# The last expert place's rows by one-hot products, other rows summed while it runs, and a second mixer that begins block of tokens by block

## The chip, the cores and the metric

One core of a Trainium2 chip runs the whole program as one launch. The metric is device time in microseconds (us), lower is better. All arithmetic is fp32 in effect: most matrix products are made as three products of fp32r halves (a high part `h` and a low part `l` of each operand: h·h, h·l, l·h), which is why every weight page is first split by a ScalarE cast (`wh`) and a VectorE subtraction (`wl`).

## The reference, cut to what matters

Two blocks follow each other on 512 tokens of 1024 features. The part around the change is the end of the first block (32 experts, 4 per token) and the beginning of the second block's mixer:

```python
# first block: mixture of experts on h2 = rms_norm(x) * (1 + scale2) + shift2
gates = softmax(top_k(h2 @ w_router + b_router, 4))
for each expert e, for its tokens:
    gu = xe @ w_gate_up[e] + b_gate_up[e]
    g, u = minimum(gu[:, :D_FF], 7.0), clip(gu[:, D_FF:], -7.0, 7.0)
    y = ((u + 1.0) * (g * sigmoid(1.702 * g))) @ w_down[e] + b_down[e]
x = x + gate2 * (sum over a token's 4 experts of gate * y)

# second block: mixer
h = rms_norm_2(x, mix_norm_g)
u, q, k, v, f_logit, g_ssm, g_att = split(h @ w_in)
y_ssm = s5_branch(u, ...)                       # a scan over the tokens
y_att = forgetting_attention(norm(q), norm(k), v, f_logit, ...)
x = x + (sigmoid(g_ssm) * y_ssm + sigmoid(g_att) * y_att) @ w_out
x = x + peer_ffn(rms_norm_2(x), ...)
```

## The kernel before

The program has four phases, one after the other. Tokens lie in four blocks of 128 (`NB` = 4, `tb` 0 to 3), features in eight chunks of 128 (`KC`). Buffers of 4 KB per partition ("pages", 128x1024) come from one pool of 30, and a load or a result waits until a page is free.

**Phase 1** (first mixer) is put in order by a planner: `race` takes a number of generators (lanes) and emits next from the one whose engines are free first by its own clock. A further lane or another page held changes the order of all of them.

**Phase 2** (experts) streams 32 experts' weights from memory in a fixed order of 24 ticks per expert: each tick uses one page of weights (the gate/up and down products `gu`, `dn`), and `at(tick, function)` hangs further work on a tick. An expert's tokens are gathered by an indirect DMA from `h2d` into a tile `xg` (there are four, `xgs`), and its scaled rows `y` are scattered by an indirect DMA on GpSimd's queue to `ybuf` in DRAM, four places per token (`Expert.finish`, line 1304; its DMA at L1317). Behind the last expert stands a run-time loop for tokens beyond an expert's 128 places (`Overflow.rest`, L1515, the loop at L1519). It runs zero times here, but all engines and DMAs meet at its end: this is the barrier between the phases, and it needs the last scatter landed.

**Phase 3** (second mixer) begins behind that barrier. SyncE's queue issues 16 loads of 512 KB of `yk` (the rows in `ybuf`, four for each block of tokens; `expert_rows`, L1573) and then weight pages `wr` (L213). ScalarE's queue issues four small loads, `grow`, `qkg`, `fb`, `causal`. `combine` adds each block's four rows to `x` (`x2[tb]`), partly on GpSimd and partly on VectorE, and ScalarE squares the sum. `roots` makes the reciprocal root of the norm by 13 operations on 128x1 (tiles `nsq`, `nr0v`, `nr0a`, `nrs`), `norm` makes `xn`, `turn` transposes it on TensorE (`xnT`) and casts the high parts `hTh`, `lows` makes the low parts `hTl`. The string `START` is the order in which these are written: a = combine, r = roots, n = norm, t = turn, l = lows, w = the first weight split. Then come four chunks of `u` and one of the forget logits (all named `ft`, 24 products of 512 columns each), and then `weave`, which interleaves lanes by the rates in `W3`: the scan (`ssm_scan`: products `x` and `y`, `zr`, `zi`, `tmp`), two attention lanes (`qt`, `s`, `pt`, `ob`), and `pair(qr)` for four quarters of the heads. `pair(qr)` waits until quarter `qr` - 2 has been attended, makes q, k and v of its two heads (`qkv(i, qr)` with i = 0, 1, 2: 96 products of 256 columns each), and then the two gate chunks (`ft`). For i = 0 and 1 `qkv` ends with a norm on VectorE (`qssq`, `rqv`, `rqa`, `qrs`, `raw`). Behind the weave follow `z` and `wo`.

**Phase 4** is the PEER layer, which the change doesn't touch.

GpSimd prepares the scan's rotations (`pw`, `co`, `si`, 12 operations on 128x512) as soon as its own adds are done.

Of the kernel before, what the change touches and what calls it, by code (L numbers as in the profile page):

```python
# [18 lines left out]
P = 128  # L19
# [286 lines left out]
def phase1(K):  # L306
# [693 lines left out]
    nc.scalar.dma_start(out=br, in_=row_bcast(I["b_router"], NE))  # L1000
    B, A = [pair_b(h) for h in range(4)], [pair_a(p) for p in range(4)]
    race(K.clock, third(0), third(1), third(2), third(3), prefetch(), roots(0), roots(1), *[second(tb) for tb in range(NB)], ws.lane(WSA), split_out(), norms(), *(lane(B[0],A[0]),lane(B[1],A[1]),lane(B[2],A[2]),lane(B[3],A[3])), lane(chunks(), projects()), lane(mod_rows((0, 1, 2)), mod_rows((3,))), mods2())
# [16 lines left out]
START = "a0 r01 n0 t0 a1 l0 r12 n1 t1 a2 l1 r23 n2 t2 a3 l2 w0 r34 n3 t3 l3"  # L1019
# [4 lines left out]
SMALL = 0.07  # L1024
EXTRA = (5, 7)
# [190 lines left out]
class Expert:  # L1216


    def __init__(self, K, xg, rank, mv, rows, sel):
        self.K, self.xg, self.rank, self.mv, self.rows = K, xg, rank, mv, rows  # L1220
        self.sel = sel
# [7 lines left out]
    def lists(self):  # L1229
# [13 lines left out]
        nc.vector.tensor_scalar(self.tok, self.dst, 2, None, op0=ALU.logical_shift_right)  # L1243
        nc.gpsimd.indirect_dma_start(out=self.xg, out_offset=None, in_=K.h2d[:, :],  # L1244
# [59 lines left out]
    def finish(self, last=False):  # L1304
        K, nc = self.K, self.K.nc
        y = K.page(name="y")
# [8 lines left out]
        if FIN == 2 and not last:  # L1315
            nc.gpsimd.tensor_tensor(out=y, in0=y, in1=K.gate2, op=ALU.mult)
        st = nc.gpsimd.indirect_dma_start(out=self.rows, out_offset=bass.IndirectOffsetOnAxis(ap=self.dst[:, :1], axis=0),  # L1317
                                          in_=y, in_offset=None, bounds_check=4 * T - 1, oob_is_err=False)
        for o in (K.scat or []):
            K.tc.declare_no_dep(st.ins, o.ins, reason="rows of other (token, choice) pairs")  # L1320
        if K.scat is not None:
            K.scat.append(st)
# [52 lines left out]
def phase2(K, nexp=NE):  # L1375
# [10 lines left out]
    K.ybuf = K.drp.tile([4 * T, D], F32, name="ybuf")  # L1386
# [7 lines left out]
    def mk(e):  # L1394
        rank, mv, sel = (K.rank, K.mv, K.selE) if e < FIXED else (K.rank_p, K.mv_p, K.sel_p)
        sel = sel[:, e:e + 1].to_broadcast([P, P])
        ex[e] = [Expert(K, xgs[e % 3], lambda tb: rank[:, tb, e:e + 1], lambda tb: mv[:, tb, e, :], K.ybuf[:, :], sel)]
# [32 lines left out]

    for i in range(16):
        at(1 + i, step, order)
    at(16, mk, 2)
    for e in range(nexp + 1):
# [13 lines left out]
        for x in ex.get(e, []):  # L1448
# [4 lines left out]
            at(n0 + 24 + 17, x.finish, e == nexp - 1)  # L1453
        if e == 5:
# [28 lines left out]
    for _ in chain(params, db):  # L1483
        pass
    K.rank = K.mv = K.G = K.cnt = K.iota32 = K.idc = None
    K.sel_p = K.rank_p = K.mv_p = K.rank_2 = K.served = K.perm = None
    over.rest(xgs[0])


class Overflow:  # L1490
# [5 lines left out]
    def block(self, b, xg):  # L1496
# [16 lines left out]
        return Expert(K, xg, lambda tb: r4[:, tb, 0:1], lambda tb: mv[:, tb, :], K.ybuf[:, :], sel.to_broadcast([P, P]))  # L1513

    def rest(self, xg):  # L1515
        K, nc, tc = self.K, self.K.nc, self.K.tc
        K.scat = None
        nx = nc.values_load(K.nx[0:1, 0:1], min_val=0, max_val=NXB - 1, skip_runtime_bounds_check_because="a count of blocks")
        with tc.For_i(0, nx, 1) as b:  # L1519
# [18 lines left out]
            x.finish()  # L1538

# [26 lines left out]
def expert_rows(K):  # L1566

    out = []
    for tb in range(NB):
        ys = [K.page(name="yk") for _ in range(4)]  # L1570
        src = K.ybuf[tb * 512:(tb + 1) * 512, :].rearrange("(p k) d -> p k d", k=4)
        for k in range(4):
            K.nc.sync.dma_start(out=ys[k], in_=src[:, k, :])  # L1573
        out.append(ys)
    return out


def combine(K, tb, ys, ssq):

    nc, x = K.nc, K.x2[tb]  # L1580
    nc.gpsimd.tensor_tensor(out=x, in0=x, in1=ys[0], op=ALU.add)
    nc.gpsimd.tensor_tensor(out=ys[1], in0=ys[1], in1=ys[2], op=ALU.add)
    nc.vector.tensor_tensor(out=x, in0=x, in1=ys[1], op=ALU.add)
    for i in range(2):
        s = slice(i * 512, (i + 1) * 512)
        nc.vector.tensor_tensor(out=x[:, s], in0=x[:, s], in1=ys[3][:, s], op=ALU.add)
# [269 lines left out]
def phase3(K):  # L1856
# [126 lines left out]
    for c in range(4):  # L1983
        K.split(feat_chunk(), *uT[c])
# [660 lines left out]
```

## Time and profile before

| what | us |
|---|---|
| median of 3 runs | 3761.43 |
| lowest and highest of them | 3748.43, 3765.33 |
| the profiled execution's own time | 3763.79 |
| its span (first to last instruction) | 3762.0 |
| TensorE, VectorE busy in the span | 3390.4, 3237.6 |
| last product of the last expert to first product of the second mixer | 1780.8 to 1850.5 |
| second mixer's weave | 1879.6 to about 2270 |

The profile is of one execution. A row of the timeline gives a start, a duration, engine, line, operation and tiles (out<-in), the number of like instructions in a row, and in brackets how long the engine had idled before and what released it. A row of the windows gives the busy time of TensorE (PE), its weight loads (PEld), VectorE (DVE), ScalarE (ACT) and GpSimd (POOL), each with its number of instructions, then the granted TensorE clock (1.00 is 2.4 GHz, 0.50 is 1.2 GHz), the DMA engines' share and GB/s. Products overlap, so the distance between two starts, not the duration of one, is their cost in a row. Nearly all operations are issued by one helper and so carry line 84: they are told apart by tile names. SPq, ACTq and POOLq are the engines' DMA queues.

### The profile page before, as it was taken

Reading aid. Unit: us, or ns where it says so; the run is one execution under the profiler, and the core shown is the slowest. Engines: PE = TensorE matmul, PEld = TensorE weight load, DVE = VectorE, ACT = ScalarE, POOL = GpSimd, SP = SyncE. Lnnn points to the kernel's source line nnn. Section 1 sums busy time; section 2 is a strip of 40 time slices with the busy share of each in tenths; the row PEclk is TensorE's granted clock in tenths of the full one; section 3 lists DMA queues with packets and bytes.
Section 4 is the critical chain, followed back from the end, with each engine's and each line's share of the span. In section 5 each row is a group of like instructions: output and inputs, shape, how many; then the busy total and the mean of one; then the engine's idle time right before and its main releaser. Section 6 shows DMA issues by size and latency. Waiting matters only on the chain. (4 is left out here: it accounts for less than half of the span.)

```text
span 3762.0 us, 51865 instructions
## 1 busy us (share of the span) xinstructions
PE 3390.4 (90%) x17053; PEld 2884.7 (77%) x17053; DVE 3237.6 (86%) x5729; ACT 1845.3 (49%) x2684; POOL 1096.1 (29%) x742
## 2 busy tenths in 40 slices
PE   6788789898999999999488899899889889999999
PEld 6776667667777888887377777798889889888887
DVE  7888789999898999998688776499999986799988
ACT  3233367666665677776234453333344445333333
POOL 5545501101110111111334440023223230456554
PEclk8878889999999999999699899899999999999999
DMA  6224369888997899997511112366779787999997
GB/s 216 85 85 157 129 232 327 295 306 304 334 317 252 319 356 368 351 366 282 182 51 51 51 52 100 104 208 216 237 241 309 251 291 248 334 340 342 345 340 260
DMA packets 453989, 906.05 MB, mean 241 GB/s; under 512 B 37810, under 2 KB 188978, under 8 KB 453586
## 3 DMA queue, kind: packets, MB, share of 16 engines
q1 hardware_dynamic: 333488, 692.66, 53.0%
q0 software_dynamic: 46368, 151.03, 11.1%
q10 hardware_dynamic: 73858, 59.00, 4.7%
q8 instruction: 136, 2.23, 0.2%
q14 instruction: 139, 1.14, 0.1%
HBM read 845.42 MB, written 74.96 MB: 245 GB/s over the span
## 5 line engine op out<-in xcount | busy, mean ns | idle before, releaser
L84 DVE TENSOR_TENSOR wl<-wr,wh 128x1024 fp32r<-128x1024 f32 x1106 | 1346.4, 1252 | 150.9 <-ACT wh L84 145.1
L84 ACT CAST wh<-wr 128x1024 fp32r<-128x1024 f32 x1133 | 1132.8, 1049 | 166.7 <-DVE wl L84 44.0
L84 PE MATMUL ft<-HT,wh 128*128 128x384 f32 (+1 forms) x2304 | 620.7, 350 | 4.9 <-ACT wh L84 4.9
L84 PE MATMUL out<-wh,HT 128*128 128x512 f32 x1536 | 473.3, 389 | 1.5 <-ACT HT L84 1.5
L84 PE MATMUL gu<-wl,exh 128*128 128x512 f32 x1056 | 417.6, 395 | 22.5 <-DVE wl L84 22.3
L84 PEld LDWEIGHTS ft<-HT,wh 128*128 128x128 f32 x2304 | 424.4, 193 | 14.8 <-ACT wh L84 5.5
L84 PE MATMUL ft<-HT,wl 128*128 128x384 f32 (+1 forms) x1152 | 402.8, 350 | 26.0 <-DVE wl L84 25.8
L84 PE MATMUL gu<-wh,exh 128*128 128x512 f32 x1056 | 420.6, 398 | 0.3 <-ACT wh L84 0.3
L84 PE MATMUL gu<-wh,exl 128*128 128x512 f32 x1056 | 413.7, 392 | 0.0
L84 PEld LDWEIGHTS out<-wh,HT 128*128 128x128 f32 x1536 | 288.2, 188 | 61.9 <-ACT HT L84 1.8
L2454 POOL DMA_INDIRECT ug<-in_peer_u,et x128 | 167.6, 1309 | 453.5 <-DVE sv L84 241.5
L84 PE MATMUL out<-wl,HT 128*128 128x512 f32 x768 | 298.8, 389 | 0.0
L2454 POOL DMA_INDIRECT ug<-in_peer_v,et x128 | 156.3, 1221 | 362.0 <-DVE x L84 240.0
L84 PEld LDWEIGHTS gu<-wl,exh 128*128 128x128 f32 x1056 | 199.5, 189 | 74.8 <-DVE wl L84 35.6
L84 PEld LDWEIGHTS ft<-HT,wl 128*128 128x128 f32 x1152 | 221.8, 193 | 40.7 <-DVE wl L84 35.6
L1317 POOL DMA_INDIRECT ybuf<-y,dst x33 | 93.3, 2827 | 505.1 <-DVE y L84 505.1
L84 PE MATMUL qkv<-wl,hTh 128*128 128x256 f32 (+1 forms) x736 | 227.2, 309 | 14.4 <-DVE wl L84 11.8
L1244 POOL DMA_INDIRECT xg<-h2d,tok x33 | 42.9, 1300 | 675.8 <-PE dn L84 478.1
L84 PE MATMUL qkv<-wh,hTh 128*128 128x256 f32 (+1 forms) x736 | 235.1, 319 | 2.0 <-ACT wh L84 2.0
L84 PEld LDWEIGHTS gu<-wh,exh 128*128 128x128 f32 x1056 | 199.8, 189 | 45.7 <-ACT wh L84 3.0
L84 PE MATMUL dn<-wl,ath 128*128 128x512 f32 x528 | 213.5, 404 | 22.9 <-DVE wl L84 20.2
L84 PEld LDWEIGHTS gu<-wh,exl 128*128 128x128 f32 x1056 | 199.3, 189 | 41.8
(481 smaller groups left out, 6952.8 us busy)
## 6 DMA issues: line engine op xcount, KB each, us to landing
wr<-in_w_gate_up SPq DMA_DIRECT2D x512, 512.0 KB, 6.5
wr<-in_w_down SPq DMA_DIRECT2D x256, 512.0 KB, 6.4
wr<-in_u_t SPq DMA_DIRECT2D x128, 512.0 KB, 4.3
wr<-in_peer_v SPq DMA_DIRECT2D x128, 512.0 KB, 6.1
wr<-in_w_in SPq DMA_DIRECT2D x68, 512.0 KB, 3.5
wada<-in_w_ada SPq DMA_DIRECT2D x48, 512.0 KB, 4.3
Sd<-us ACTq DMA_DIRECT2D x128, 192.0 KB, 4.7
Gd<-gst ACTq DMA_DIRECT2D x12, 2048.0 KB, 15.7
```

Of the source, the lines that this page charges most:

```text
L84: return f(*a, **kw)
L1244: nc.gpsimd.indirect_dma_start(out=self.xg, out_offset=None, in_=K.h2d[:, :], in_offset=bass.IndirectOffsetOnAxis(ap=self.tok[:, :1], axis=0),
L1317: st = nc.gpsimd.indirect_dma_start(out=self.rows, out_offset=bass.IndirectOffsetOnAxis(ap=self.dst[:, :1], axis=0), in_=y, in_offset=None ...
L2454: nc.gpsimd.indirect_dma_start(out=r, out_offset=None, in_=tab, in_offset=bass.IndirectOffsetOnAxis(ap=et[:, m:m + 1], axis=0), bounds_che ...
```

## The change

1. **Zeros.** A lane of phase 1 fills one page with zeros and writes it 16 times (512 KB each, on SyncE's queue, paced 15 planner units apart) over `ybuf`, which is now made in phase 1. A place of `ybuf` that nobody scatters to therefore reads as zero.
2. **The last expert.** Its one-hot matrix is transposed by four TensorE transposes and a ScalarE copy into `xgs[3]`, its scaled rows go to `xgs[2]`, and its scatter is gone. Its part of each block's sum comes from fp32 products of the one-hot with the rows (`spread`, tiles `lt`, two products of 512 columns for each block).
3. **Loads ahead of the barrier.** In the last expert's ticks SyncE loads the rows of blocks 0 and 1 (`wind_up`), and VectorE adds them (`add_rows`): block 0's four ahead of the last `y`, block 1's four behind it and ahead of the barrier.
4. **Behind the barrier** the stream of phase 3 is made earlier (`stream3`): two weight pages, block 2's rows, two weight pages, block 3's rows, then the rest.
5. **`START`** is rewritten, with p = products, a = add the products and square, b = add the loaded rows, q = the q and k products of quarter 0 for one block of tokens, v = the first four `wl`. All adds are VectorE's.
6. **Order of the mixer.** Quarter 0's q, k and v stand ahead of the `u` chunks and the forget chunk and out of the weave; `pair(0)` makes its gates alone. The rates `W3` are unchanged.

VectorE from the last expert's down product to the first transposed block. `dn` is the down product, `yk` the loaded rows, `x` the sum of a block. Before:

```order
L84 SCALAR_TENSOR_TENSOR y_17256<-dn_17180,gate_16898,gate_3055 128x512
L1519 REGISTER_ALU
L1519 COMPARE_AND_BRANCH
L1519 UNCONDITIONAL_BRANCH
L84 SCALAR_TENSOR_TENSOR gq_17308<-qkg_17304 128x1
L84 TENSOR_TENSOR x_3047<-x_3047,yk_17273 128x1024
L84 TENSOR_TENSOR x_3047<-x_3047,yk_17275 128x512 x2
L84 TENSOR_TENSOR nsq_17333<-nssq_17324 128x1
```

The same place after, ahead of the barrier (the second fence stands behind it, at `gq`):

```order
L84 TENSOR_TENSOR x_3168<-x_3168,yk_16781 128x1024
L84 SCALAR_TENSOR_TENSOR xg_4130<-dn_16823,gate_15842,gate_3183 128x512
L84 SCALAR_TENSOR_TENSOR xg_4130<-dn_16824,gate_15842,gate_3183 128x512
L84 TENSOR_TENSOR x_3170<-x_3170,yk_16786 128x1024
L84 TENSOR_TENSOR x_3170<-x_3170,yk_16787 128x1024
L84 TENSOR_TENSOR x_3170<-x_3170,yk_16788 128x1024
L84 TENSOR_TENSOR x_3170<-x_3170,yk_16789 128x1024
L1568 TENSOR_LOAD nx_5761
```

```order
L84 SCALAR_TENSOR_TENSOR gq_17372<-qkg_17368 128x1
L84 TENSOR_TENSOR x_3168<-lt_17406,x_3168 128x512
L84 TENSOR_TENSOR x_3168<-lt_17407,x_3168 128x512
L84 TENSOR_TENSOR x_3170<-lt_17410,x_3170 128x512
L84 TENSOR_TENSOR x_3170<-lt_17411,x_3170 128x512
L84 TENSOR_TENSOR nsq_17432<-nssq_17384 128x2
```

VectorE's eight adds of blocks 0 and 1 have moved ahead of the barrier, and block 0's roots now stand behind the adds of eight products.

TensorE behind the barrier, before (`xnT` the transposes, `ft` the first `u` chunk):

```order
L1519 UNCONDITIONAL_BRANCH
L84 MATMUL xnT_17352<-ident_68,xn_17349 128x128 x4
L84 MATMUL xnT_17359<-ident_68,xn_17349 128x128 x4
...
L84 MATMUL xnT_17497<-ident_68,xn_17487 128x128 x4
L84 MATMUL ft_17521<-hTh_17312,wh_17465 128x512
```

and after (`xg` here are the last expert's rows and the one-hot, `qkv` the q and k products of the first block of tokens):

```order
L84 MATMUL lt_17406<-xg_4130,xg_4131 128x512
...
L84 MATMUL lt_17419<-xg_4130,xg_4131 128x512
L84 MATMUL xnT_17451<-ident_68,xn_17448 128x128 x4
L84 MATMUL xnT_17458<-ident_68,xn_17448 128x128 x4
L84 MATMUL xnT_17472<-ident_68,xn_17469 128x128 x4
L84 MATMUL xnT_17479<-ident_68,xn_17469 128x128 x4
L84 MATMUL qkv_17503<-wh_17386,hTh_17376 128x256
```

Eight products come ahead of the first transposes, and products of 256 columns begin when two blocks of tokens are transposed, not four.

TensorE in the first quarter's attention inside the weave, before (`pt` transposes the weights, `ob` multiplies them by v):

```order
L84 MATMUL pt_18733<-ident_68,e_18517 128x128
L84 MATMUL qkv_18616<-wh_18618,hTh_17316 128x256
L84 MATMUL qkv_18616<-wl_18619,hTh_17316 128x256
...
L84 MATMUL qkv_18617<-wh_18618,hTl_17319 128x256
L84 MATMUL ob_18725<-pt_18731,vh_18205 128x512
```

and after:

```order
L84 MATMUL pt_19015<-ident_68,spare_18125 128x128 x2
L84 MATMUL ob_18960<-pt_19007,vh_17934 128x384
...
L84 MATMUL pt_19051<-ident_68,spare_18125 128x128 x2
L84 MATMUL y_19058<-tmp_19009,cz_9111 32x512
L84 MATMUL y_19058<-tmp_19024,cz_9295 32x512
L84 MATMUL x_19064<-u_17941,bt_8329 128x512 x2
```

The 36 `qkv` products that stood between the transposes and the products with v are gone from there; between the last gate chunk and the end of this attention only the scan's `x` and `y` products stand beside it.

The diff, cut to its core:

```diff
+    def zeros():
+        z = K.page(name="zero")
+        v.memset(z, 0.0)
+        for i in range(16):
+            yield ZPACE * (i + 1)
+            nc.sync.dma_start(out=K.ybuf[i * P:(i + 1) * P, :], in_=z)
...
-START = "a0 r01 n0 t0 a1 l0 r12 n1 t1 a2 l1 r23 n2 t2 a3 l2 w0 r34 n3 t3 l3"
+START = "w0 p0 p1 p2 p3 a0 a1 r02 n0 t0 v0 n1 t1 l0 b2 a2 l1 q0 b3 a3 r24 n2 t2 q1 n3 t3 l2 l3 q2 q3"
...
+            for tb in range(NB):
+                nc.tensor.transpose(b[:, tb * P:(tb + 1) * P], self.ohs[:, tb, :].bitcast(F32), K.ident)
+            nc.scalar.copy(self.late[1], b)
...
+        if self.late is not None:
+            return
         st = nc.gpsimd.indirect_dma_start(out=self.rows, ...)
...
+    def spread(self, tb):
+        y, ohT = self.late
+        bs = [self.K.bank("lt") for _ in range(2)]
+        for i, b in enumerate(bs):
+            self.K.nc.tensor.matmul(b, ohT[:, tb * P:(tb + 1) * P], y[:, i * 512:(i + 1) * 512], start=True, stop=True)
+        return bs
...
+    def wind_up():
...
+        for tb in range(2):
+            rows[tb] = expert_rows(K, tb)
+    def add_rows(tb):
+        for y in rows.pop(tb):
+            nc.vector.tensor_tensor(out=K.x1[tb], in0=K.x1[tb], in1=y, op=ALU.add)
...
+        if e == nexp - 1:
+            at(n0 + 22, wind_up)
+            at(n0 + 24 + 8 + 6, add_rows, 0)
...
+    K.late = ex[nexp - 1][0]
+    add_rows(1)
     over.rest(xgs[0])
+    stream3(K)
+    for tb in range(2, NB):
+        for _ in range(2):
+            K.ws3.load()
+        rows[tb] = expert_rows(K, tb)
...
-def combine(K, tb, ys, ssq):
-    nc.gpsimd.tensor_tensor(out=x, in0=x, in1=ys[0], op=ALU.add)
-    nc.gpsimd.tensor_tensor(out=ys[1], in0=ys[1], in1=ys[2], op=ALU.add)
...
+    def total(tb):
+        x, sq = K.x2[tb], K.page(name="sq")
+        for i, b in enumerate(last.pop(tb)):
+            s = slice(i * 512, (i + 1) * 512)
+            nc.vector.tensor_tensor(out=x[:, s], in0=b, in1=x[:, s], op=ALU.add)
+            nc.scalar.activation(sq[:, s], x[:, s], AF.Square, accum_out=ssq[:, tb, i:i + 1])
...
+    for i in range(3):
+        for _ in qkv(i, 0):
+            pass
     up = [K.page(F32R, [P, 2, T], name="u") for _ in range(4)]
...
-        for i in range(3):
+        for i in range(3 if qr else 0):
             yield from qkv(i, qr)
```

## Rows read from the trace of the kernel before

**Rows 1.** Windows by stage; columns as told above.
```profile
0.00:500.00 500.00, 379.95 (x2154) 329.17 (x2154) 397.15 (x786) 176.28 (x374) 258.76 (x148) 0.82 0.39 134
1780.00:1850.00 70.00, 8.04 (x33) 5.98 (x32) 50.23 (x88) 10.17 (x29) 37.91 (x23) 0.54 0.52 187
```
**Rows 2.** Timeline of the seam between the phases.
```profile
1780.13 1.43 DVE L84 SCALAR_TENSOR_TENSOR y<-dn,gate,gate 128x512 f32<-128x512 f32 x2 [4.56 <-PE dn L84]
1781.83 0.98 POOL L1317 DMA_INDIRECT ybuf<-y,dst  x1 [15.72 <-DVE y L84]
1785.87 0.34 ACTq L1861 DMA_DIRECT2D grow<-in_mix_g_row  x1
1850.52 0.78 PE L84 MATMUL ft<-hTh,wh 128*128 128x512 f32 x1
```
**Rows 3.** Timeline: the tail of the last expert.
```profile
1758.73 7.39 POOL L1317 DMA_INDIRECT ybuf<-y,dst  x1 [32.66 <-DVE y L84]
1769.80 5.77 DVE L84 TENSOR_TENSOR wl<-wr,wh 128x1024 fp32r<-128x1024 f32 x5 [0.25 <-ACT wh L84]
```
**Rows 4.** DMA, 1757 to 1770 (GB/s in 40 slices), then issues with us to landing.
```profile
GB/s 416 378 416 340 366 340 315 353 403 416 403 416 403 403 403 403 378 202 63 38 0 0 0 0 25 0 0 0 0 101 429 378 202 101 0 0 0 50 0 0
ybuf<-y,dst POOLq DMA_INDIRECT x1, 9.6
yk<-ybuf SPq DMA_DIRECT2D x16, 512.0 KB, 9.0
grow<-in_mix_g_row ACTq DMA_DIRECT2D x1, 512.0 KB, 5.4
qkg<-in_qk_g ACTq DMA_DIRECT2D x1, 1.0 KB, 7.3
```
**Rows 5.** Timeline: adds (one of 1024, two of 512 columns) and a cast, GpSimd idle.
```profile
1832.51 2.55 DVE L84 TENSOR_TENSOR x<-x,yk 128x1024 f32<-128x1024 f32 x3
1843.39 1.03 ACT L84 CAST wh<-wr 128x1024 fp32r<-128x1024 f32 x1
```
**Rows 6.** Tile gm: fp32 products in phase 1 (min/median/max ns; first and last start).
```profile
L84 PE MATMUL gm<-gate,onesF x4: 592/592/644, 409.9 to 411.2; 128*128 128x512 f32 x4
```
**Rows 7.** Window: the clock some 3.5 us after dense products begin at 1850.5.
```profile
1854.00:1856.00 2.00, 2.00 (x10) 1.66 (x9) 1.17 (x1) 0.80 (x1) 0.00 (x0) 1.00 1.04 387
```
**Rows 8.** Timeline: roots and low parts beside GpSimd's operations, and alone.
```profile
1805.18 1.43 DVE L84 TENSOR_TENSOR nsq<-nssq 128x1 f32<-128x1 f32 x1 [0.79 <-ACT yk L84]
1815.48 3.18 DVE L84 SCALAR_TENSOR_TENSOR xn<-x,nrs,grow 128x512 f32<-128x512 f32 x2
1823.20 1.51 POOL L84 TENSOR_TENSOR tmp<-pw,pw 128x512 f32<-128x512 f32 x1
1823.71 1.40 DVE L84 TENSOR_TENSOR hTl<-xnT,hTh 128x256 fp32r<-128x256 f32 x4
1845.59 0.15 DVE L84 TENSOR_TENSOR nsq<-nssq 128x1 f32<-128x1 f32 x1
1848.09 1.41 DVE L84 SCALAR_TENSOR_TENSOR xn<-x,nrs,grow 128x512 f32<-128x512 f32 x2
```
**Rows 9.** Timeline: the first products of quarter 0, 24 in a row.
```profile
1879.59 0.28 PE L84 MATMUL qkv<-wh,hTh 128*128 128x256 f32 x1
...
1882.34 0.28 PE L84 MATMUL qkv<-wh,hTl 128*128 128x256 f32 x1
```
**Rows 10.** The weave: a VectorE group, first and last row of one norm, two windows.
```profile
L84 DVE TENSOR_TENSOR wl<-wr,wh 128x1024 fp32r<-128x1024 f32 x35 | 48.8, 1393 | 10.2 <-ACT wh L84 10.2
1899.68 1.27 DVE L84 TENSOR_REDUCE qssq<-tmp 128x4 f32<-128x512 f32 x2
1909.52 1.23 DVE L84 TENSOR_TENSOR raw<-raw,qrs 128x1024 f32<-128x1024 f32 x1
1880.00:1940.00 60.00, 48.22 (x296) 41.76 (x296) 53.47 (x73) 16.12 (x22) 19.46 (x16) 0.89 0.15 45
1940.00:2270.00 330.00, 306.36 (x1747) 249.34 (x1747) 253.40 (x450) 150.87 (x260) 140.33 (x98) 0.95 0.18 52
```

More of the change, by code (lines that the diff above doesn't have):

```diff
@@ L1305, in finish @@
         K, nc = self.K, self.K.nc
-        y = K.page(name="y")
+        y = self.late[0] if self.late is not None else K.page(name="y")
         for i in range(2):
@@ L1538, in rest @@
             x.finish()
+            for tb in range(NB):
+                for i, b in enumerate(x.spread(tb)):
+                    s = slice(i * 512, (i + 1) * 512)
+                    nc.vector.tensor_tensor(out=K.x1[tb][:, s], in0=b, in1=K.x1[tb][:, s], op=ALU.add)
 def down_bias(K):
@@ L1853, in norm_T, with stream3 @@
     return xn
-def phase3(K):
-    nc, I, tc = K.nc, K.I, K.tc
-    K.open_phase(K.ctx3, 3)
-    K.x2 = K.x1
-    grow = K.page(name="grow")
-    nc.scalar.dma_start(out=grow, in_=row_bcast(I["mix_g_row"], D))
-    rows = expert_rows(K)
-    qkg = K.small([P, 2], tag="qkg", bufs=1)
-    nc.scalar.dma_start(out=qkg, in_=I["qk_g_2"])
-    fb = K.const([40, 1], name="fb")
-    nc.scalar.dma_start(out=fb, in_=I["fbias"])
-    gq = K.const([P, 1], name="gq")
-    nc.vector.scalar_tensor_tensor(gq, qkg[:, 0:1], P ** -0.5, qkg[:, 1:2], op0=ALU.mult, op1=ALU.mult)
-    causal = K.const([P, T], name="causal")
-    nc.scalar.dma_start(out=causal, in_=I["causal"])
-    hT = [(K.page(F32R, [P, 2, T], "hTh"), K.page(F32R, [P, 2, T], "hTl")) for _ in range(4)]
-    def hTk(k):
-        return hT[k // 2][0][:, k % 2, :], hT[k // 2][1][:, k % 2, :]
+def stream3(K):
+    I = K.I
     w2 = I["w_in_2"]
@@ L1898, in phase3 @@
     UC, QC, KC0, VC, GS, GA = 0, 512, 1536, 2560, 3592, 4616
[L1899 removed]
+    srcs = []
     for qr in range(4):
@@ L1906, in phase3, with hTk @@
     srcs += [I["w_out_2"][k * P:(k + 1) * P, :] for k in range(KC)]
-    ws = WStream(K, srcs, 2, 1, late=True)
-    ws.load()
-    ws.load()
+    K.ws3 = WStream(K, srcs, 4, 4, late=True)
+def phase3(K):
+    nc, I, tc = K.nc, K.I, K.tc
+    K.open_phase(K.ctx3, 3)
+    K.x2 = K.x1
+    grow = K.page(name="grow")
+    nc.scalar.dma_start(out=grow, in_=row_bcast(I["mix_g_row"], D))
+    qkg = K.small([P, 2], tag="qkg", bufs=1)
+    nc.scalar.dma_start(out=qkg, in_=I["qk_g_2"])
+    fb = K.const([40, 1], name="fb")
+    nc.scalar.dma_start(out=fb, in_=I["fbias"])
+    gq = K.const([P, 1], name="gq")
+    nc.vector.scalar_tensor_tensor(gq, qkg[:, 0:1], P ** -0.5, qkg[:, 1:2], op0=ALU.mult, op1=ALU.mult)
+    causal = K.const([P, T], name="causal")
+    nc.scalar.dma_start(out=causal, in_=I["causal"])
+    hT = [(K.page(F32R, [P, 2, T], "hTh"), K.page(F32R, [P, 2, T], "hTl")) for _ in range(4)]
+    def hTk(k):
+        return hT[k // 2][0][:, k % 2, :], hT[k // 2][1][:, k % 2, :]
+    ws = K.ws3
     ssq, rs, xn = K.small([P, NB, 2], tag="nssq"), K.small([P, NB], tag="nrs"), {}
@@ L1958, in phase3 @@
         else:
-            {"n": norm, "t": turn, "l": lows}[op[0]](tb)
-    rows = None
+            {"p": products, "a": total, "n": norm, "t": turn, "l": lows, "q": queries}[op[0]](tb)
+    late = K.late = K.add_rows = None
     for tb in range(NB):
```

132 lines of the change are left out of this document (76 added, 56 removed).

## The prediction, made before the changed kernel was run

> **What bounds the kernel now.** I read the windows by stage first. The experts run with TensorE nearly always busy; the hole is the seam between the phases, where TensorE has 8.04 us of work in 70 at a mean clock of 0.54 [rows 1]. The timeline says why: the last rows `y` come at 1780.13, their scatter is issued at 1781.83, and the loads of phase 3 begin only at about 1785.9, when it has landed; from there a chain on VectorE and GpSimd (adds, roots, norm) runs until the first dense product at 1850.52 [rows 2]. The later weave, 1880 to 2270, is the second stage to read: in its first 60 us VectorE is busy 53.5 and TensorE 48.2, afterwards TensorE 306 of 330 [rows 10]. Two engines share the bound there, so work taken out of it is worth less than its TensorE time.
>
> **The last expert's tail and the barrier.** The scatter of the last but one expert starts at 1758.73 [rows 3] and lands 9.6 us later [rows 4], at 1768.3. The row loads of blocks 0 and 1 read what it writes and go then; memory is idle (the GB/s fall to nothing ahead of it [rows 4]). 8 x 0.524 MB at the 0.41 MB/us of the same line are 10.2 us, so block 0 lands at about 1775 and block 1 at 1780. VectorE ends its last weight pages at 1769.80 + 5.77 = 1775.57 [rows 3]: block 0's adds find their data. One add of 128x1024 costs what a `wl` does, 5.77 / 5 = 1.15 us [rows 3], or 1.27 by the adds themselves [rows 5]; I take 1.2. Four end at 1780.4, `y` (1.43 [rows 2]) at 1781.9, block 1's four at 1786.7; with half a microsecond for the branch the barrier falls at 1787.2, against 1785.8 before: +1.4. The removed scatter is thus paid for by the adds, and nothing is gained here. Queued behind the adds on VectorE is `y` itself, and behind `y` the products: if the rows came late, these would wait one for one.
>
> **Behind the barrier.** 16 product instructions (8 fp32 products of two). The nearest rows are fp32 products of phase 1: four starts from 409.9 to 411.2, 0.43 us apart at full clock [rows 6], so 6.9 us at 2.4 GHz and 13.9 at 1.2. TensorE has idled some 6 us; at 1850.5 a dense run that began at the low clock had 2.4 GHz again by 1854 [rows 7]. I take 9: products end at 1796.3. `qkg` lies over `xgs`, which the products read, so its load can't be issued before; 7.3 us to landing [rows 4] put `gq` at 1803.6, and `gq` stands ahead of all of VectorE's adds. On ScalarE's queue `grow` (5.4 us [rows 4]) and `causal` wait for pages, and four casts (1.03 [rows 5]) stand ahead of the squares; the weight pages are loads 1, 2, 7 and 8 of 12 in SyncE's row, 4.2 MB or 10 us, so the casts end at about 1804.6, no later than `gq`. Then a0 and a1, four adds of 0.7 (half of 1.27 and a little), and squares: 1808.
>
> The roots come next, and GpSimd decides their price. Block 0's 13 small operations took 1805.18 to 1815.48 beside GpSimd's adds, 10.3 us; block 3's, alone, 1845.59 to 1848.09, 2.5 [rows 8]. The adds on GpSimd are gone, but its 12 rotation operations (about 1.3 us each, by the one of 1.51 [rows 8]; some 16 us in all) now start when the products end, at 1796, and last to 1812. So the roots (now of two blocks at once) are slowed for 4 us and end at 1814; bounds 1810.5 and 1818. `xn` 1.41 [rows 8], four `wl` 4.6 and the second `xn` 1.41 bring 1821.5, low parts half a microsecond more: q0 starts at about 1822.5.
>
> The adds of a0 and a1 read PSUM and SBUF. Four `hTl`, also one input from each, took 1.40 us at 1823.71 while GpSimd's `tmp` ran [rows 8], 0.35 apiece, so I charge no contention to them. The Trainium skill says the same in "SBUF — State Buffer", section "Who interferes with whom": an instruction of VectorE with at most one SBUF input does not contend with GpSimd, one with two contends with a GpSimd instruction that reads SBUF, and whoever comes second is blocked for the whole instruction. By that rule the trace's slow roots and quick `hTl` agree, and the rule speaks against the place of the rotations here. Were it wrong and the four adds as slow as the first `xn` (3.18 for two [rows 8]), the chain would be 3.6 us longer.
>
> Then VectorE has block 2's adds 4.8, a2 1.4, l1 1.4, block 3's 4.8, a3 1.4, a square 1, roots 2.5, `xn` 1.4: 18.7 us from the end of l0 at 1823.3, so 1842; block 2's transposes on TensorE stand ahead of q1, which begins at 1843.5 and stays dense. Products of 256 columns are (1882.34 - 1879.59) / 23 = 0.12 us apart [rows 9]. q1 to q3 are 144 of them, 17.3 us, with 1.7 for the low clock at the start and 2.5 for the transposes of block 3: 1865. Quarter 0's v, 96 x 0.12 = 11.5: 1876.5. Five `ft` chunks took 1850.52 to 1879.59 [rows 2, 9], 29.1 with their slow start, so 27.4 now: 1904. The weave, which began at 1879.6, begins 24.4 us later.
>
> **What the weave loses.** TensorE: 288 x 0.12 = 34.5 us. VectorE: six `wl` of 1.39, 8.4 [rows 10]; two norms, of which one took 1899.68 to 1910.7, 11.0, and needs at least its sums and its last product, 2.5 [rows 10]; two v splits 1.4: between 15 and 32, the middle 23. Were TensorE the bound all through, the weave would be 34.5 shorter; were it VectorE, 23. By the windows the first 60 us are VectorE's and the other 330 TensorE's by a little [rows 10]; I take 28.
>
> **Small terms.** Four transposes and a copy in the last experts: +1, since TensorE is full there. Phase 1: the zeros are 16 loads' worth of traffic in a stretch with the DMA engines busy 0.39 [rows 1], so hidden; the page and the lane reorder the planner's work, where TensorE has 380 of 500 us [rows 1]. No row prices that: 8 us either way by two or three waits for a page, taken at 0.
>
> **Sum.** +24.4 - 28 + 1 = -2.6. Against the profiled execution's 3763.8 that is 3761.2; it stands 2.4 above the median, so I predict 3758.8.
>
> **The rivals.** (1) *TensorE bounds the whole weave and the chain is quick.* Roots by the lower bound and products at full clock bring q1 some 5 us forward, and the weave gives back all 34.5: 24.4 - 5 - 34.5 + 1 = -14, 3747. With the block additions overlapped better as well (block 2's rows land long before 1823), another 6: 3741. For it: TensorE's 306 of 330 [rows 10]. Against: the first 60 us. Chance 0.25, of which 0.2 under 3742.6.
>
> (2) *The first attention runs unfilled* (the other side). Between quarter 0's `pt` and `ob` stood 180 `qkv` products, 21.6 us, by the order above; now quarter 1's are used up before and quarter 2 waits for this very attention, so only the scan's products stand there and TensorE waits for VectorE's rounds. If all of that stays open, the weave is only 34.5 - 21.6 = 13 shorter: +24.4 - 13 + 1 = +12, 3774. The point from which it decides: slower as soon as the weave gives back less than the 25.4 that the seam and the transposes cost. With the chain at its late bounds as well (products 5 more, roots 4 more) 3783. For it: VectorE's share in the first 60 us [rows 10], which this stretch resembles. Chance 0.3, half of it above 3780.
>
> (3) *Phase 1 moves by its own reordering*: 8 us either way, 3751 or 3767. Chance 0.1.
>
> (4) *It doesn't do what it says*: the row loads land late. Were each batch of four to need 9.0 us [rows 4] one after the other, block 1 would land at 1786.3 and the barrier at 1791: 3763. Chance 0.05.
>
> **How the numbers follow.** The forecast holds the remaining 0.3, and 3758.8 is its time; rivals 3 and 4 surround it within 0.5% (18.8 us, about what a measurement of this kernel can tell from no change). Faster by more: 0.2; slower by more: 0.15; within: 0.65. The range reaches from 3740, the quick end of rival 1, to 3782, the slow end of rival 2, and leaves out about 0.1 on either side.
>
> **What would show it.** Right: a barrier at about 1787, the first `qkv` near 1822, dense products from about 1844, the first scan products `x` at about 1904, and 28 us less from there to `z`. Wrong: rows that land behind `y`; roots that are quick or wait for `gq` longer; a weave that shrinks by 34 or by 13; a first expert product that is moved by more than a few microseconds in phase 1, which no row here prices.

## The result, and the profile after

The changed kernel takes **3787.01 us** (median of 15 runs) against 3761.43 (15 runs): a ratio of **1.0067, interval 1.0055 to 1.0080**. It is 25.6 us slower. I had forecast 3758.8 and a range from 3740 to 3782. In the ratios below, one execution of 10685 us (in the run that releases quarter 2 earlier) is left out.

For every kernel below I read three lengths from its trace: from the start of the last expert's last down product to the start of the forget chunk's first VectorE operation (the **seam**), from there to the first `z` product (the **weave**), and the rest. These are the rows of the changed kernel for it, a tile's instructions with count, min/median/max ns, first and last start:

```profile
L84 PE MATMUL dn<-wh,atl x48: 387/390/396, 1702.3 to 1774.4; 128*128 128x512 f32 x48
L84 DVE TENSOR_SCALAR fp<-ft,fb x1: 742/742/742, 1907.3 to 1907.3; 40x512 f32<-40x512 f32 x1
L84 PE MATMUL z<-u,wh x115: 387/390/505, 2298.7 to 2339.9; 128*128 128x512 f32 x115
```

So the seam is 132.9 us and the weave 391.4. Before, the same rows give 1780.4, 1879.8 and 2281.8: 99.4 and 402.0. The seam grew by 33.5, the weave shrank by 10.6, together **+22.9**.

The profile's spans differ by 27.2 (3789.2 and 3762.0). The other 4.3 can't be put down to the change: the last expert product came 6.0 earlier, and a stretch of phase 4 whose instructions are the same was 10.6 longer (520.8 and 531.4 from its first `G` to its first `out` product). Each kernel here was profiled once; over these profiles that stretch varies from 515.6 to 533.2, and the start of the last expert product from 1769.7 to 1786.9, with no pattern by edit that I can see. The seam varies too: five kernels whose seam is the changed kernel's own gave 129.9 to 132.9. Most of that lies ahead of the barrier (taken as SyncE's first issue behind it), which fell 6.4 to 8.4 us behind the start of the last expert product. From the barrier to the forget chunk the five gave 123.0 to 124.5, so small gains in the seam are read from there.

The seam, in the timeline of after, to be held beside [rows 2, 3, 8]:

```profile
1771.20 5.00 DVE L84 TENSOR_TENSOR x<-x,yk 128x1024 f32<-128x1024 f32 x4
1776.12 1.40 DVE L84 SCALAR_TENSOR_TENSOR xg<-dn,gate,gate 128x512 f32<-128x512 f32 x2
1777.44 4.99 DVE L84 TENSOR_TENSOR x<-x,yk 128x1024 f32<-128x1024 f32 x4
1782.81 0.95 SPq L213 DMA_DIRECT2D wr<-in_w_in  x2
1783.18 10.10 PE L84 MATMUL lt<-xg,xg 128*128 128x512 f32 x16 [8.37 <-DVEq L1569]
1794.79 0.33 ACTq L1941 DMA_DIRECT2D qkg<-in_qk_g  x1
1801.61 0.61 DVE L84 SCALAR_TENSOR_TENSOR gq<-qkg 128x1 f32<-128x1 f32 x1 [19.18 <-DMA yk<-ybuf]
1805.45 0.28 DVE L84 TENSOR_TENSOR nsq<-nssq 128x2 f32<-128x2 f32 x1 [0.83 <-ACT sq L84]
1818.19 0.56 PE L84 MATMUL qkv<-wh,hTh 128*128 128x256 f32 x1
1838.09 0.56 PE L84 MATMUL qkv<-wh,hTh 128*128 128x256 f32 x1
1866.17 0.58 PE L84 MATMUL qkv<-wl,hTh 128*128 128x256 f32 x1 [8.58 <-DVE wl L84]
```

The rows show block 0's four adds end at 1776.2, 1.4 us behind the last down product, so that `y` (named `xg` here) waits for them. The products for the last expert take 10.1 us. `gq` holds VectorE until 1801.6: its bracket names the row loads, but `qkg`, which it reads, was issued at 1794.8 and took 6.7 us to land. The first dense products (q0 and q1) come at 1818.2 and 1838.1. The last row is new: TensorE waits 8.6 us for a `wl` at the second product of quarter 0's v.

The weave, in windows of before and of after (PE, PEld, DVE, ACT, POOL busy, clock, DMA share, GB/s), to be held beside [rows 10]:

```profile
1879.80:2281.80 402.00, 366.58 (x2097) 299.84 (x2095) 316.06 (x534) 170.11 (x289) 164.31 (x116) 0.94 0.19 54
```
```profile
1907.30:2298.70 391.40, 341.59 (x1808) 268.23 (x1807) 288.63 (x496) 157.95 (x272) 157.32 (x116) 0.90 0.18 49
1987.00:2007.00 20.00, 20.00 (x100) 15.79 (x99) 17.50 (x35) 13.24 (x24) 8.10 (x6) 1.00 0.27 79
2007.00:2027.00 20.00, 11.53 (x34) 6.61 (x32) 13.36 (x23) 10.39 (x19) 8.70 (x8) 0.60 0.09 26
2027.00:2047.00 20.00, 15.34 (x62) 8.81 (x61) 14.40 (x22) 4.27 (x8) 12.05 (x11) 0.80 0.00 1
```

TensorE has 289 instructions fewer, 34.5 us by [rows 9], but is busy only 25.0 less and idle 14.4 longer (49.8 instead of 35.4). The holes are in the first attention: 34 products in 20 us, and neither VectorE (13.4) nor any other engine is full there. The granted clock in that window is 0.60, so what is left takes longer as well. That the missing 9.5 of busy time are the lower clock (0.90 instead of 0.94 over the weave) is an inference from these rows, not measured alone. Before, the first attention (its transposes begin at 1985.5) had about 100 products or more in 20 us, and the emptiest 20-us window of the weave had TensorE 15.19 busy:

```profile
1980.00:2000.00 20.00, 15.53 (x103) 14.05 (x103) 16.80 (x35) 12.50 (x21) 2.52 (x1) 0.83 0.09 27
2000.00:2020.00 20.00, 18.47 (x128) 15.72 (x127) 18.28 (x29) 5.72 (x11) 8.80 (x8) 1.00 0.09 27
```

The waits of the weave say what TensorE waits for (us in total, times, longest), before and after:

```profile
PE ob L84 <- DVE pt L84: 10.7, 6, 5.5
```
```profile
PE ob L84 <- DVE pt L84: 23.6, 11, 6.7
PE ob L84 <- ACT pt L84: 5.0, 1, 5.0
```

It is the product of attention weights with v (`ob`) that waits for `pt`, mostly for VectorE's part of it; the one wait for ScalarE's part, 5.0 us, lies in the window with the 34 products. This is a chain inside one head. That other products used to cover it is the reading of these rows, tested below.

### The profile page after: what moved, and what is told of

Its sections match the earlier page's. It is cut to its first block, busy times and chain, and to the rows that moved or that the text cites. A ratio compares the mean times of both kernels' runs of the same rounds, so it can differ in the third digit from the quotient of the medians.

```text
span 3789.2 us, 51872 instructions
## 1 busy us (share of the span) xinstructions
PE 3400.8 (90%) x17073; PEld 2887.0 (76%) x17073; DVE 3215.8 (85%) x5716; ACT 1844.7 (49%) x2684; POOL 1068.0 (28%) x733
```

## Which part costs it

Theory: the order of the mixer costs some 30 us and the seam gains a few. Rivals: the seam itself is slower, the zeros disturb phase 1, or phase 4's 10 us belong to the change.

**The seam alone.**

```diff
-START = "... n1 t1 l0 b2 a2 l1 q0 b3 a3 r24 n2 t2 q1 n3 t3 l2 l3 q2 q3"
+START = "... n1 t1 l0 b2 a2 l1 b3 a3 r24 n2 t2 n3 t3 l2 l3"
...
-    for i in range(3):
-        for _ in qkv(i, 0):
-            pass
...
-        for i in range(3 if qr else 0):
+        for i in range(3):
```

> The changed kernel with its mixer in the order of before: u chunks and the forget chunk first, quarter 0's q, k and v inside the weave again; zeros, products for the last expert, early row loads and sums stay. Theory A (the loss lies in the mixer's order): dense products begin at about 1842 instead of 1850.5, the weave is as long as before (402 us from the end of the forget chunk to z), and the time is 3761 - 4 (the part up to the last expert, which was 4 earlier in the changed kernel) - 4 (the seam) = 3753 (0.998). Rival B (the loss lies in the seam and what follows from it, or in phase 4): 3770 or more (1.002 or more).

Measured: **0.9984 (0.9969 to 0.9999)**, seam 93.6, weave 401.8. The seam gains 5.8 us, and the weave is what it was.

**The mixer's order alone**, in the kernel before:

```diff
+    for i in range(3):
+        for _ in qkv(i, 0):
+            pass
     up = [K.page(F32R, [P, 2, T], name="u") for _ in range(4)]
...
-        for i in range(3):
+        for i in range(3 if qr else 0):
```

> The kernel before with the mixer's order alone: quarter 0's q, k and v written ahead of the u chunks and out of the weave, behind the transposes of all four blocks; scatter, barrier and adds as before. Theory A (the order of the mixer costs some 30 us whatever the seam is): from the last expert product to the forget chunk 99.4 + 34.5 + 8 = 142, the weave 391, the time 1.0085. If the block-wise q products in the changed kernel are worth their place in the hole, this kernel is slower than the changed one by the 5.8 us of q0 and by the seam's 5.8: 1.0067 + 0.003 = 1.0097. Rival B (the two parts work against each other, and the order alone costs little): 1.003 or less.

Measured: 1.0073 (1.0051 to 1.0094), seam 136.2, weave 391.8. The same 391 as in the changed kernel, with the old barrier, scatter and adds: the loss is the order's, and the two parts add up to a little less than the changed kernel's 524.3 (136.2 + 391.8 - 5.8 = 522.2). The 1.0097 that I expected for the slower seam did not come: here TensorE waited 2.3 us in all for a `wl` in quarter 0, not 8.6.

**The zeros alone**, in the kernel before:

```diff
+        z = K.page(name="zero")
+        v.memset(z, 0.0)
+        for i in range(16):
+            yield 15.0 * (i + 1)
+            nc.sync.dma_start(out=K.ybuf[i * P:(i + 1) * P, :], in_=z)
```

> The kernel before with the zeros alone: one page filled and written 16 times in phase 1, which reorders the planner's work there. Theory A (the last expert came 4 us earlier in the changed kernel because phase 1 was reordered): 3757 (0.999), the last `y` near 1776. Rival B (the 4 us came from elsewhere, or from chance): 3761 to 3764 (1.0 to 1.0007), the last `y` near 1780. Its phase 4 is a second sample of unchanged work there: if the 10.6 us that phase 4 was longer in the changed kernel's profile are chance, they may show here as well.

Measured: 1.0004 (0.9988 to 1.0019), seam 98.9, weave 402.6. Phase 1 is not moved by more than this can tell. Its last expert product began at 1786.9, later than in either kernel and not earlier as theory A asked, and its phase 4 stretch took 528.2 with nothing changed there: such differences come without the change.

## The wait in quarter 0's v

**v first, norms behind it.**

```diff
-    for i in range(3):
+    for i in (2, 0, 1):
         for _ in qkv(i, 0):
```

> The changed kernel (3787) with one edit: behind the q and k products of quarter 0, its v products are written first and the q and k norms behind them, so that VectorE splits v's weights ahead of the norms. In the changed kernel TensorE waited 8.6 us there for a `wl` behind the two norms. Theory A (that wait moves everything behind it): the weave begins 8 us earlier and the time falls by 8 to 9, to 3778 (ratio to the kernel before 1.0045). Rival B (the weave is bound by VectorE, which has the same work either way): the weave begins earlier but lasts as much longer, 3785 to 3788 (1.0065 to 1.007).

Measured: 1.0051 (1.0034 to 1.0068), seam 130.3, weave 390.7. Neither: the wait only moved. The second u chunk's `wl` now stood behind both norms, and TensorE waited 6.8 us there (its weight load 7.2) instead of 8.6. The seam of 130.3 lies among the 129.9 to 132.9 of kernels with the seam unchanged; from the barrier it is 121.9 against 123.0 to 124.5, so at most 1.1 to 2.6 us came off. The total can't tell the two forecasts apart.

**v first, one norm behind each of the first two u chunks.**

```diff
+    for _ in qkv(2, 0):
+        pass
...
         K.split(feat_chunk(), *uT[c])
+        for _ in (qkv(c, 0) if c < 2 else ()):
+            pass
```

> The changed kernel with quarter 0's v products first and its two norms written one behind the first and one behind the second u chunk. In the run with v first the wait only moved: the second u chunk's low part then stood behind both norms (7.2 us). Theory A (the 8.6 us are a matter of where the norms stand on VectorE's queue): no wait of TensorE over 2 us between the last q product and the forget chunk, that stretch is 8 us shorter than in the changed kernel, 3779 (1.0045). Rival B (the weave takes up what comes earlier): the same stretch is shorter, but the weave longer, 1.006 or more.

Measured: 1.0058 (1.0035 to 1.0080), seam 125.5, weave 391.7. From the barrier to the forget chunk it is 117.2 us, some 7 less than the 123.0 to 124.5 with the norms ahead, and the two other runs with this edit alone in their seam gave 116.5 and 117.1. The weave did not take it up; the total can't show it (its interval spans 1.0035 to 1.0080). TensorE's waits in that stretch are 3.2 us in two, the longer 2.3: near to what theory A asked for, and not quite under its 2.

## Why the weave gave back so little

The weave's lanes advance by numbers, `W3`: a rate for the lane of q, k, v and gates, a rate and a start for each attention lane, a rate for the scan. Each step moves a lane on by 1 / its rate, and the lane that is least far on goes next. The change took 29 of the first lane's some 180 steps away and left the numbers, so at 184 that lane comes to its end early against the others.

**Attention at once.**

```diff
-W3 = (184, 160, 0.15, 160, 0.18, 150)
+W3 = (184, 160, 0.0, 160, 0.03, 150)
```

> The changed kernel with one line changed: the two attention lanes of the weave start 0.15 earlier in its pacing (0.0 and 0.03 instead of 0.15 and 0.18), since quarter 0's q, k and v are ready when the weave begins. Theory A (TensorE idles because the first attention runs without other products beside it while quarter 2 waits for it): the first attention now runs beside quarter 1's products, the weave is 10 to 18 us shorter, 3769 to 3777 (1.002 to 1.004). Rival B (VectorE bounds the weave's first part, so nothing is won by an earlier start): 3784 to 3790 (1.006 to 1.0075).

Measured: 1.0113 (1.0090 to 1.0136), weave 407.6. Both theories fell. Attention ended at 2282.6, and the scan alone was left behind it until `z` at 2318.8:

```profile
2282.60:2318.80 36.20, 15.78 (x26) 4.23 (x25) 22.31 (x28) 1.15 (x2) 16.54 (x12) 0.55 0.00 0
```

26 products in 36 us, with no engine full, at a granted clock of 0.55, near the lower level. The holes had moved to the end.

**Quarter 2 released earlier.**

```diff
-        while not {2 * qr - 4, 2 * qr - 3} <= {-4, -3, -2, -1, *attended}:
+        while not {2 * qr - 4, 2 * qr - 3} <= {-4, -3, -2, -1, *(turned if qr == 2 else attended)}:
```

> The changed kernel with quarter 2's q, k and v released when the heads of quarter 0 have been transposed, and no longer when they have been attended. Theory A (the first attention runs unfilled because quarter 2 waits for its end): quarter 2's products stand beside it, no 20-us window of the weave has TensorE under 14 busy, the weave is 10 to 18 us shorter than 391, 3769 to 3777 (1.002 to 1.004). Rival B (the lane then runs dry later, beside the second attention, which gives the gain back): within 4 us of the changed kernel, 1.0055 to 1.008.

Measured: 1.0086 (1.0060 to 1.0113), weave 398.6. Where the first attention had its holes, there now stood products, and the holes opened 100 us later beside the second attention (windows of this run):

```profile
2010.80:2030.80 20.00, 16.38 (x117) 14.56 (x115) 15.24 (x24) 14.64 (x24) 4.84 (x5) 1.00 0.20 53
2110.80:2130.80 20.00, 10.95 (x30) 6.58 (x28) 12.92 (x18) 4.60 (x8) 5.39 (x5) 0.67 0.00 0
```

This is what rival B describes, beyond the size that it allowed. So the wait for the release is not what the weave's length hangs on. That the filling work is used up too soon, whoever releases it, is what the next runs test.

**That lane slower.**

```diff
-W3 = (184, 160, 0.15, 160, 0.18, 150)
+W3 = (154, 160, 0.15, 160, 0.18, 150)
```

> The changed kernel with one number changed: the rate of the weave's lane that makes q, k, v and gates is 154 instead of 184, since quarter 0's q, k and v (some 29 of its 180 steps) have left that lane; at 184 it runs ahead of the first attention and then waits for it. Theory A (the weave gives back only 10 of 34 us because this lane is used up before the first attention): products stand beside the first attention again, no 20-us window of the weave has TensorE under 14 busy, the weave falls from 391 to 375 to 383, the time to 3771 to 3780 (1.002 to 1.005). Rival B (the weave's length is set by VectorE and by chains inside attention and scan, whatever stands beside them): 388 to 394, 1.006 to 1.0075.

Measured: 1.0040 (1.0023 to 1.0058), weave 383.1. 8 us came back, at the edge of what theory A forecast. Now this lane was last: from 2271.9 the run's window shows TensorE full, mostly with gate products, and the other engines under half.

```profile
2271.90:2291.90 20.00, 20.00 (x91) 15.40 (x91) 7.43 (x11) 9.43 (x13) 0.00 (x0) 1.00 0.18 54
```

**A rate between, with the norms moved** (on top of the edit of the run with the norms between):

```diff
-W3 = (184, 160, 0.15, 160, 0.18, 150)
+W3 = (164, 160, 0.15, 160, 0.18, 150)
```

> The changed kernel with v first and the norms between the u chunks (alone 7 us shorter from the last expert product to the forget chunk: 125.5 instead of 132.9) and the rate of the q, k, v and gate lane at 164 (at 154 the weave was 383 instead of 391, but its last 20 us were gate products alone). Theory A (the loss is a matter of pacing and of one wait, both mendable): 125.5 + 378 = 503.5 from the last expert product to z, as in the kernel before (501.4): 1.000 to 1.002. Rival B (with 34.5 us of products gone the weave can't be filled, at whatever rate): weave 383 or more, 1.003 or more.

Measured: 1.0020 (1.0006 to 1.0034), seam 123.3, weave 384.6: 507.9 together, between the two forecasts. This rate is no better for the weave than 154, and by the weave alone the rival seemed right.

**Attention earlier and slower, that lane slower**, on top of the run with the norms between:

```diff
-W3 = (184, 160, 0.15, 160, 0.18, 150)
+W3 = (160, 150, 0.08, 150, 0.11, 150)
```

> The changed kernel with v first and the norms between the u chunks, and the weave paced anew: attention begins at 0.08 and 0.11 instead of 0.15 and 0.18 and runs at 150 instead of 160, the lane of q, k, v and gates at 160 instead of 184. Theory A (pacing can win the rest back: attention spread over a longer stretch leaves fewer holes): weave 365 to 378, ratio 0.997 to 1.001. Rival B (the weave is held by chains and by VectorE in whichever pacing): 383 to 395, 1.003 to 1.006.

Measured: **0.9981 (0.9964 to 0.9998)**, seam 125.5, weave **368.8**. The weave gives back 33.2 of the 34.5 us. Its window:

```profile
1898.70:2267.50 368.80, 328.54 (x1809) 260.52 (x1808) 299.12 (x498) 155.70 (x269) 158.63 (x116) 0.94 0.18 51
```

The instructions are as many as in the changed kernel; TensorE is idle 40.3 instead of 49.8, busy 13 less, and the clock is 0.94 again. `ob` waits 14.4 us for VectorE's `pt`, not 23.6. One hole is left, a new one near the beginning, where the scores `s` wait for `qT`:

```profile
1947.90 0.69 PE L84 MATMUL s<-qT,qT 128*128 128x128 f32 x2 [11.00 <-DVE qT L84]
```

**The same pace, nothing else**, in the changed kernel:

```diff
-W3 = (184, 160, 0.15, 160, 0.18, 150)
+W3 = (160, 150, 0.08, 150, 0.11, 150)
```

> The changed kernel with the weave's pace alone changed (attention from 0.08 and 0.11 at 150, the lane of q, k, v and gates at 160), the norms where the change put them. Theory A (the weave gave back only 10 of 34 us because its pace was kept; the wait of v's weights is a second, separate 7 us): weave 368 to 372, stretch from the last expert product to the forget chunk 132 to 133, 1.000 to 1.0015. Rival B (the pace works only with the norms moved, which changes what stands at the weave's start): weave 380 or more, 1.003 or more.

Measured: 1.0006 (0.9988 to 1.0023), seam 130.0, weave 369.8. The pace alone brings 21.6 us of weave back; it needs nothing from the norms. Set side by side, the weave has three lengths and little spread: 401.8 to 402.6 in five kernels with the old order and pace, 390.7 to 391.8 in four with the new order and the old pace, 368.8 to 369.8 in three with the new order and the new pace.

**The same attention pace in the kernel before:**

```diff
-W3 = (184, 160, 0.15, 160, 0.18, 150)
+W3 = (184, 150, 0.08, 150, 0.11, 150)
```

> The kernel before with the attention lanes' pace of the run with both paced (from 0.08 and 0.11 at 150), its lane of q, k, v and gates left at 184, since that has all its work. Theory A (the pace fits the new order, in which quarter 0 is ready when the weave begins, and the old pace fitted the old one): weave 400 to 410, 0.999 to 1.002. Rival B (the pace is better whatever the order, and what it won in the changed kernel says nothing of the order): weave 390 or less, 0.997 or less.

Measured: 1.0032 (1.0015 to 1.0048), weave 415.6, which is 13.6 longer than with its own pace. Both forecasts were too short. For the attention lanes, the pace is not simply better: it fits the order in which quarter 0 is ready beforehand. With its q, k, v lane left at 184 it is not the whole pace of the other run, and the whole pace in the kernel before was not run.

## The seam's own chain

**Small loads, gq and first casts moved back**, in the kernel with the seam alone: the casts (w0) behind the first block's transposes, the three loads behind all that `START` writes, `gq` behind the forget chunk.

```diff
-START = "w0 p0 p1 p2 p3 a0 a1 r02 n0 t0 v0 ..."
+START = "p0 p1 p2 p3 a0 a1 r02 n0 t0 w0 v0 ..."
...
     late = K.late = K.add_rows = None
+    nc.scalar.dma_start(out=qkg, in_=I["qk_g_2"])
+    nc.scalar.dma_start(out=fb, in_=I["fbias"])
+    nc.scalar.dma_start(out=causal, in_=I["causal"])
...
+    nc.vector.scalar_tensor_tensor(gq, qkg[:, 0:1], P ** -0.5, qkg[:, 1:2], op0=ALU.mult, op1=ALU.mult)
```

> The run with the seam alone (0.9984 of the kernel before), and in it the loads of qkg, fb and causal, the operation gq and the four first casts moved behind the norm of the first block. In the changed kernel VectorE's first adds behind the barrier waited for gq until 1802 though the products had ended at 1793, and the squares for the four casts until 1803. Theory A (this queue order holds the chain by some 8 us): first roots at about 1797 after a barrier at 1783, dense products 6 to 8 us earlier than in the run with the seam alone, 3752 (0.9965). Rival B (the roots then run beside GpSimd's rotations and are slowed to the same end, or the transposed block waits for weights): within 2 us of the run with the seam alone, 0.998 to 0.999.

Measured: 0.9994 (0.9976 to 1.0012), seam 92.7; from the barrier to the forget chunk 85.3, as in the kernel with the seam alone (85.3). The seam alone: the barrier, the first of the 13 operations of the roots, what follows them on VectorE:

```profile
1787.63 1.02 SPq L213 DMA_DIRECT2D wr<-in_w_in  x2
1810.72 0.84 DVE L84 TENSOR_TENSOR nsq<-nssq 128x2 f32<-128x2 f32 x1 [2.29 <-ACT sq L84]
1814.91 1.42 DVE L84 SCALAR_TENSOR_TENSOR xn<-x,nrs,grow 128x512 f32<-128x512 f32 x2
1816.24 4.63 DVE L84 TENSOR_TENSOR wl<-wr,wh 128x1024 fp32r<-128x1024 f32 x4
```

And this run, with the last operation of the roots and one of GpSimd's beside them:

```profile
1784.51 1.02 SPq L213 DMA_DIRECT2D wr<-in_w_in  x2
1798.20 1.04 DVE L84 TENSOR_TENSOR nsq<-nssq 128x2 f32<-128x2 f32 x1 [7.24 <-ACT sq L84]
1801.55 1.05 POOL L84 TENSOR_TENSOR tmp<-pw,pw 128x512 f32<-128x512 f32 x1
1807.35 1.11 DVE L84 SCALAR_TENSOR_TENSOR nrs<-nr0a,nrs 128x2 f32<-128x2 f32 x1
1808.49 1.41 DVE L84 SCALAR_TENSOR_TENSOR xn<-x,nrs,grow 128x512 f32<-128x512 f32 x2
1812.92 4.63 DVE L84 TENSOR_TENSOR wl<-wr,wh 128x1024 fp32r<-128x1024 f32 x4 [3.02 <-ACT wh L84]
```

Behind the barrier the roots began 9.4 us earlier (13.7 instead of 23.1), and `xn` followed 3.3 earlier (24.0 instead of 27.3), since the roots took 10.3 us and not 4.2. In the changed kernel, where GpSimd was nearly through, they took 4.4, and alone 2.5 [rows 8]. The other 3.3 were lost at once: VectorE's `wl` waited 3.0 us for the casts that this edit had put behind the first norm, and began 28.4 us behind the barrier instead of 28.6. The rival held: the queue order was the visible wait, and behind it stood GpSimd's rotations and the casts.

**Block 2's rows added in VectorE's hole**, on top of that:

```diff
-START = "p0 p1 p2 p3 a0 a1 r02 n0 t0 w0 v0 n1 t1 l0 b2 a2 l1 b3 ..."
+START = "p0 p1 p2 p3 a0 a1 b2 r02 n0 t0 w0 v0 n1 t1 l0 a2 l1 b3 ..."
```

> The run with the quick seam, and in it block 2's four loaded rows added while VectorE waits for the squares of blocks 0 and 1 (it idled 7.2 us there) instead of behind the first low parts. Theory A (VectorE's work behind the first norm sets the first dense product, so 5 us moved into a hole come off): dense products 60 us behind the last expert product instead of 64.4, ratio 0.998. Rival B (the adds have two inputs from SBUF and stand beside GpSimd's rotations, or the rows have not landed, and the roots start later by what is saved): 64 to 66 us, 0.999 to 1.0.

Measured: **0.9977 (0.9964 to 0.9990)**, seam 89.4, first dense product at 60.9 (1841.2 - 1780.3). The four adds took 6.58 instead of 5.00 us, partly beside GpSimd, and still the first dense product came 3.0 us earlier behind the barrier (54.0 instead of 57.0); in the nine kernels that begin with the same `START`, q0 included, that stretch to q0 differs by 1.4 (33.95 to 35.38).

**All that helped**, in the changed kernel, on top of the norms between the u chunks and the loads and `gq` moved as above:

```diff
-W3 = (184, 160, 0.15, 160, 0.18, 150)
+W3 = (160, 150, 0.08, 150, 0.11, 150)
...
-START = "w0 p0 p1 p2 p3 a0 a1 r02 n0 t0 v0 n1 t1 l0 b2 a2 l1 q0 b3 ..."
+START = "p0 p1 p2 p3 a0 a1 b2 r02 n0 t0 w0 v0 n1 t1 l0 a2 l1 q0 b3 ..."
```

> The changed kernel with all that helped: norms between the u chunks, the pace of the run with both paced, and at the seam the small loads, gq and the first casts behind block 0's norm and block 2's rows added in VectorE's hole. Theory A (the parts add): 125.5 - 4.2 = 121.3 from the last expert product to the forget chunk, weave 369, 490 in all against 501.4 before: 0.997. Rival B (the quick seam is taken up by q0, which fills the same hole, or by late weights): 125 and 369, 0.998 or more.

Measured: **0.9982 (0.9967 to 0.9996)**, seam 121.4, weave 369.1: 490.5 together, where 490 was worked out, against 501.4 before. The sum came out, but not by an earlier q0: it began 36.0 us behind the barrier, no earlier than in the changed kernel (35.4). The gain is at q1, 50.9 instead of 55.3 us behind the barrier. With block 2's rows already added, TensorE waits half as long for that block's `xn`, in the changed kernel and here:

```profile
1836.47 1.97 PE L84 MATMUL xnT<-ident,xn 128*128 128x128 f32 x8 [11.53 <-DVE xn L84]
```
```profile
1836.49 1.97 PE L84 MATMUL xnT<-ident,xn 128*128 128x128 f32 x8 [5.55 <-DVE xn L84]
```

Four kernels here lie below the kernel before with their whole interval: the seam alone (by 0.0001), the paced one (by 0.0002), the one with adds in the hole, and this one. Their intervals overlap, so none is shown to be the best.

## Why the prediction was wrong

- **The seam's chain came out, in part by errors that cancelled.** From the last expert product's start I had 42.1 us to q0 and 63.1 to q1; measured were 43.8 (1818.2 - 1774.4) and 63.7. The barrier came 1.6 later than forecast, since block 0's adds ended 1.4 us behind the down product (in the four other kernels with the same code up to there and an unchanged seam it fell 0.4 us earlier than forecast to 0.6 later); the branch, for which I had 0.5 without a row, took 0.4. The products took 10.1 for 9, and the roots began 3.4 late; but they took 4.4 for 6.
- **q1 to the weave was missing a wait.** I had 60.5 us of dense work and it took 69.2. The step "Quarter 0's v, 96 x 0.12" assumed weights that were split: I priced the two norms as work that leaves the weave, without asking what stood behind them on VectorE's queue at their new place. v's first `wl` did, and TensorE waited 8.6. Behind that wait, 22 products started 0.21 us apart, not 0.12.
- **The weave's term failed.** I took 28 between two engines' losses, 23 (VectorE) and 34.5 (TensorE). VectorE's loss was 27.4 (316.06 to 288.63), inside the 15 to 32 that I gave it, and yet the weave shrank by 10.6. The bound was neither engine's total but the order in which the lanes were interleaved, and that order's numbers had been left as they were: with other numbers alone, the changed kernel's weave was 369.8, so 32.2 came back. That the pace was kept while work was taken out stood in the change's list ("the rates are unchanged"), and no step of mine priced it.
- **Rival 2 was the right place and half the mechanism.** The first attention did run unfilled, and a weave 13 shorter (measured 10.6) is near what came. But its reason, that quarter 2 waits for this attention, was not what held the weave: released earlier, the holes moved to the next attention and the weave was 7.2 longer. That the size came near is thus partly luck. Its sum of 12.4 falls short of the measured 22.9 by 9.1 in the seam, mostly v's wait, and by 2.4 in the weave, less 1 for the transposes. I gave it 0.3.
- **The range was too narrow on that side.** Its upper end, 3782, held the unfilled attention with a late chain (9 us). No term held a wait inside the dense products, which cost as much, with a chain that was nearly in time. The base of 3761.4 with the measured 22.9 gives 3784.
- **Rivals 1, 3 and 4**: TensorE did not bound the weave (idle 49.8 us of 391.4); the zeros alone showed no move of phase 1 that could be told from what executions differ by; the row loads came in time (block 0's adds began at 1771.2, when the last weight page was split).
- The rule from "SBUF — State Buffer" in the Trainium skill, section "Who interferes with whom", held for the adds: the four from PSUM behind `gq` (the roots stand behind the adds of four products, not of eight as I wrote under the change) took 0.62 us apiece beside GpSimd, 2.47 in all. For the roots I had left out a condition. The section's sentence on one SBUF input holds outside VectorE's 2-port modes, and it counts `tensor_scalar` among the operations that can use them. Three of the 13 operations are of that kind, and one of them, `nr0v<-nsq` on 128x2, took 0.98 us beside GpSimd in the changed kernel and 0.17 alone. Which mode it ran in, no run here shows.

## What to carry to other kernels

Work that is taken out of a hand-paced interleaving may be worth its engine time only when the pace is set anew. Here 34.5 us of products gave back 10.6 with the old numbers and 32.2 with new ones. Kept, the numbers used the remaining filler up early and left chains bare, and the holes moved, to the next head or to the end, when only the start of attention or the release was corrected. Before placing a step "beside" other work, list what comes after it on the same in-order queue and who waits for that. And when a wait is taken away, look for what had been hidden behind it on the engine's neighbour.

## What the runs showed of the hardware

Thirteen dependent operations of VectorE on 128x2 elements took 2.6 us alone, some 0.16 each, and 10.3 us beside GpSimd operations of 1.05 to 1.27 us on tiles in SBUF: nine of them took 0.90 to 1.11 us, the other four still 0.16 or 0.17 (both from the run with the small loads moved back). An add of 128x1024 went only from 1.25 to 1.65 us, partly beside such operations. Small operations in a dependent row lost most here; that each of them waits for a GpSimd operation to end is the likely reason, and was not tested.
